# The first norm of a hybrid layer: its vector folded into the projection's weights, its row scale into the results

## The chip, the core and the metric

The kernel runs on one core of a Trainium2 chip. The time is that of the device for one execution, in microseconds (us), from the first to the last instruction and what little lies around them. The core has five engines with a queue each: TensorE (PE) for matrix products, VectorE (DVE), ScalarE (ACT), GpSimd (POOL) and SyncE (SP), which issues most of the loads.

## The reference

One layer over 1024 tokens of width 1024, all in float32. Only the first part matters here:

```
h = RMSNorm(x) * mix_norm              # per token: x * rsqrt(mean(x^2) + eps), times a vector of 1024
z = h @ W_in                           # columns: gq, gk, gv, gr, low-rank gate, sq, sk, sv
group A: gated linear attention in chunks of 64 (4 heads), per-head RMSNorm, SiLU(gr) gate
group B: sliding-window attention (window 128), per-head RMSNorm of sq and sk, ALiBi, sinks
x = x + concat([o_A, o_B]) @ W_out
x = x + W_down(SiLU(a) * b),  [a, b] = causal_conv3(RMSNorm(x) @ W_up)
```

## The kernel before

Tokens are cut into 8 tiles of 128 (index t), the width into 8 blocks of 128 (index k). Every float32 product is made of three products of rounded numbers: an operand is split into a rounded part `hi` and the difference `lo`, and TensorE adds hi\*hi, hi\*lo and lo\*hi. So a tile of a projection, `dense`, is 8 x 3 = 24 products of 128x512 into one PSUM bank. The split of a weight block is a rounding copy on ACT (`act.copy`) and a difference on POOL, or on DVE where `engs` says so; `piece` splits the two blocks of one load. The v blocks are the exception: DVE makes their rounding copy (`hi_eng`).

The opening: `load_x` brings tile t of x; `norm1_stat` squares and sums its rows on ACT (for tile 0 half of it on DVE), makes the row scale `r` (affine on DVE, power on POOL in `rms_scale`), and multiplies x by `r` and by the norm's vector in place (two DVE operations of 128x512). The vector comes as one row and is spread over the partitions by four small products into PSUM (`mix_ps`), from which ACT copies it later (`mix_copy`). `norm1_tr` transposes the normalized tile, 8 blocks by TensorE, and `norm_tr` splits the result into `big` (ACT copy, DVE difference). Then come the products of the q weights (`unit_q_part`, `unit_q`).

The stages follow each other as q, k (with the low-rank gate's columns), v, g, r, each over all 8 tiles, with the attention parts of both groups laid in between. Weight blocks live in nine slots (`w_tile`) that the stages use in turn, so that a block of the next stage can be split when the last product of an earlier stage has used its slot. Loads go through three buffers (`raw_tile`).

The order: every step is put into a list with a time by hand (`at(time, f, ...)`), and the list is run in the order of these times; the framework then places the instructions of each engine with a simulated timeline of its own, so an engine's queue can differ from the list in places. Each engine works off its queue in order.

What uses z afterwards: `q_post` and `kvl_post` (per-head norm with `head_rms`, then a multiply), a copy for the values (`kvl_post`, `unit_v`), `gla_qk` (times decays) and `gate` (SiLU).

## Time and profile before

| | us |
|---|---|
| median of 3 runs | 1093.66 (1092.42 to 1098.78) |
| the profiled execution, its own time | 1095.48 |
| its span, first to last instruction | 1093.8 |
| TensorE busy in the span | 1079.5 |
| DVE, POOL, ACT busy | 797.0, 641.5, 480.6 |

The mean granted clock of TensorE is 0.996 of full speed. All times of rows are from the profiled execution, counted from the first instruction. TensorE's busy time holds products at either clock. A line such as L89 is a line of the kernel; the lines of `split` (L86 to L89) serve all splits, so the tile's name tells which one it is (qw, kw, vw: weight blocks; big: transposed x).

### The profile page before, as it was taken

The page shows a single profiled execution, that of the slowest core. Times are in us where ns is not written, and L with a number is a line of the kernel's source. Part 1 is how long each engine was busy: PE and PEld are TensorE (multiplying, and loading weights), DVE is VectorE, ACT ScalarE, POOL GpSimd, SP SyncE. Part 2 cuts the span into 40 slices and gives each one's busy share as a digit, 9 for nine tenths or more (in the row PEclk, how much of TensorE's full clock was granted, in tenths as well). Part 3 has the DMA queues.
Part 4 walks back from the last instruction along what each step waited for, and adds up shares of the span by engine and source line. Part 5 has one row for each costly group of instructions (what it writes and reads, how often), then busy time and mean ns, then how long its engine had stood idle before and what let it go on. Part 6 is the DMA issues. An engine that isn't in the chain of part 4 may idle for free.

```text
span 1093.8 us, 14260 instructions
## 1 busy us (share of the span) xinstructions
PE 1079.5 (99%) x5156; PEld 867.3 (79%) x5156; DVE 797.0 (73%) x1323; ACT 480.6 (44%) x966; POOL 641.5 (59%) x518
## 2 busy tenths in 40 slices
PE   8999999999999999999999999999999999999998
PEld 5897778777788887878888888888888888888886
DVE  6646546767513268758898979797989798898965
ACT  6326656434332135445454444444444445454530
POOL 5356224233543237587878777786868697868530
PEclk9999999999999999999999999999999999999999
DMA  6124113000208201012211121212111111111104
GB/s 217 46 72 132 33 30 104 20 14 17 62 1 268 58 2 58 1 58 59 58 58 58 43 74 39 77 39 78 38 56 42 58 39 58 58 58 59 44 14 154
DMA packets 67344, 67.16 MB, mean 61 GB/s; under 512 B 4616, under 2 KB 51913, under 8 KB 67274
## 3 DMA queue, kind: packets, MB, share of 16 engines
q1 hardware_dynamic: 63432, 61.53, 18.1%
q10 hardware_dynamic: 3842, 4.73, 1.8%
q8 instruction: 41, 0.67, 0.3%
q14 instruction: 29, 0.24, 0.1%
HBM read 57.33 MB, written 4.19 MB: 56 GB/s over the span
## 4 chain that ended last, share of the span: by engine, by line
PE 93%; DVE 4%; DMA 1%; ACT 1%; issue 0%; POOL 0%; SPq 0%; ACTq 0%; POOLq 0%
PE fb L759 36%; PE dn_P L929 17%; PE do L288 7%; PE dg L288 4%; PE dr L288 4%; PE dv L288 4%; PE dq L288 3%; PE dk L288 2%; PE pv L449 1%; PE ppt L437 1%; PE dq L646 1%; PE X L759 1%; PE fb L960 1%; PE dl L960 1%; PE go L552 1%; PE go L548 1%
## 5 line engine op out<-in xcount | busy, mean ns | idle before, releaser
L929 PE MATMUL dn_P<-dw,dg 128*128 128x512 f32 x840 | 215.8, 392 | 0.0
L933 DVE TENSOR_TENSOR acc<-acc,dn_P 128x1024 f32<-128x1024 f32 x140 | 169.8, 1214 | 62.4 <-PE dn_P L929 62.3
L929 PEld LDWEIGHTS dn_P<-dw,dg 128*128 128x128 f32 x840 | 157.7, 188 | 37.1
L288 PE MATMUL do<-wow,big 128*128 128x512 f32 x384 | 93.2, 398 | 0.0
L89 POOL TENSOR_TENSOR dw<-dn,dw 128x512 fp32r<-128x512 f32 x50 | 69.0, 1380 | 33.0 <-PE dn_P L929 22.3
L288 PEld LDWEIGHTS do<-wow,big 128*128 128x128 f32 x384 | 71.1, 188 | 16.2
L426 POOL TENSOR_TENSOR pr<-pr,sm 128x1024 f32<-128x1024 f32 (+1 forms) x16 | 28.6, 1786 | 68.6 <-DVE sm L424 38.0
L759 PE MATMUL fb<-big,A11w 128*128 128x512 f32 x264 | 66.4, 396 | 0.0
L759 PE MATMUL fb<-big,A12w 128*128 128x512 f32 x264 | 65.6, 396 | 0.0
L767 DVE SCALAR_TENSOR_TENSOR ua<-fb,cc,ua 128x511 f32<-128x511 f32 x82 | 60.7, 741 | 4.2 <-ACT ua L772 3.7
L759 PE MATMUL fb<-big,S1w 128*128 128x512 f32 x240 | 60.0, 397 | 0.3 <-DVE ub L803 0.3
L759 PE MATMUL fb<-ex,S3w 128*128 128x512 f32 x240 | 59.7, 397 | 0.2 <-ACT ca L818 0.2
L759 PE MATMUL fb<-big,S4w 128*128 128x512 f32 x240 | 59.8, 396 | 0.0
L759 PE MATMUL fb<-ex,S2w 128*128 128x512 f32 x240 | 59.6, 396 | 0.0
L759 PE MATMUL fb<-ex,A22w 128*128 128x512 f32 x240 | 59.5, 397 | 0.0
L759 PEld LDWEIGHTS fb<-big,A11w 128*128 128x128 f32 x264 | 49.6, 188 | 12.0
L759 PEld LDWEIGHTS fb<-big,A12w 128*128 128x128 f32 x264 | 49.7, 188 | 11.7
L759 PEld LDWEIGHTS fb<-big,S1w 128*128 128x128 f32 x240 | 45.1, 188 | 11.7 <-issue 0.7
L759 PEld LDWEIGHTS fb<-ex,S3w 128*128 128x128 f32 x240 | 45.0, 188 | 11.6 <-ACT ca L818 0.9
L759 PEld LDWEIGHTS fb<-big,S4w 128*128 128x128 f32 x240 | 45.1, 188 | 11.0
L759 PEld LDWEIGHTS fb<-ex,A22w 128*128 128x128 f32 x240 | 45.1, 188 | 10.9
L759 PEld LDWEIGHTS fb<-ex,S2w 128*128 128x128 f32 x240 | 45.1, 188 | 10.9
(438 smaller groups left out, 2481.8 us busy)
## 6 DMA issues: line engine op xcount, KB each, us to landing
up<-in_w_up_dram SPq DMA_DIRECT2D x44, 512.0 KB, 3.9
dn<-in_w_down_dram SPq DMA_DIRECT2D x22, 512.0 KB, 3.5
acc<-in_x_dram SPq DMA_DIRECT2D x8, 512.0 KB, 7.5
out_dram<-acc SPq DMA_DIRECT2D x16, 256.0 KB, 2.0
xt<-in_x_dram SPq DMA_DIRECT2D x7, 512.0 KB, 4.7
qraw<-in_w_in_dram SPq DMA_DIRECT2D x4, 512.0 KB, 6.3
vraw<-in_w_in_dram SPq DMA_DIRECT2D x4, 512.0 KB, 4.2
qt<-qt ACTq DMA_DIRECT2D x16, 128.0 KB, 2.2
```

The lines of the kernel that those rows point to most:

```text
L89: (eng or pool).tensor_sub(lo, src, hi.bitcast(F32))
L288: pe.matmul(pb[:, :n], lhsT=big[:, t, k, ra, :], rhs=ws[k][:, rb, :n], start=(k == 0 and i == 0), stop=(k == KD - 1 and i == 2))
L426: pool.tensor_tensor(pr[:, :, s0:], pr[:, :, s0:], den[:, hs].rearrange("p (j o) -> p j o", o=1).broadcast_to((P, 4, n)), ALU.mult)
L437: pe.transpose(pb[:, j * P:(j + 1) * P], pr[:, j, b * P:(b + 1) * P], ident)
L449: pe.matmul(pb[g * 64:(g + 1) * 64, :], lhsT=vv[:, t - 1 + b, g * 64:(g + 1) * 64], rhs=pts[t, g][:, b, :], start=(b == b0), stop=(b == 1))
L548: pe.matmul(pb[:, h * P:(h + 1) * P], lhsT=a[:, lo, pr * P:(pr + 1) * P], rhs=v[:, h * P:(h + 1) * P], start=(h == 0), stop=False)
L552: pe.matmul(pb[c * 64:(c + 1) * 64, pr * 256:(pr + 1) * 256], lhsT=qt[:, pr, c * 64:(c + 1) * 64], rhs=s_st[(2 * t + c) % NS][:, pr, :], s ...
L759: pe.matmul(pb[:, ts.start * P:ts.stop * P], lhsT=w[:, ra, k, :], rhs=b_operand(bn, k, rb)[:, ts], start=(onto is None and i == 0), stop=( ...
L767: dve.scalar_tensor_tensor(dst, src, w, dst, op0=ALU.mult, op1=ALU.add)
L929: pe.matmul(pb[:, i], lhsT=g[:, ra, c:c + P], rhs=w[:, rb, :], start=(onto is None and n == 0), stop=(n == 2), skip_group_check=onto is no ...
L933: dve.tensor_add(acc, acc, pb)
L960: pe.matmul(pb, lhsT=g[:, ra, (t % 4) * P:(t % 4 + 1) * P], rhs=w[:, rb, :], start=(ch == NCH - 2 and i == 0), stop=(ch == NCH - 1 and i = ...
```

## The change

The rows of the weights are multiplied by the norm's vector when they are split, and the row scale of a token is multiplied into the results. x is transposed as loaded. In steps:

- the vector is loaded as `mixc`, 128 partitions x 8 numbers (number k of partition p is element 128k + p), from ACT's queue; the row, its four products and `mix_copy` go;
- `split` with `scale`: with `eng` given, ACT's rounding copy and DVE's difference both apply the scale; without, ACT first scales the loaded block in place and then splits it as before, with POOL's difference. The v blocks lose `hi_eng` and so are rounded on ACT;
- `norm1_stat` squares in place over the loaded x, after the transposes, and writes the row scale to `rn`, with `rn8` (times 1/8) and `rn2` (squared, over 64) beside it: two small DVE operations per tile. The two multiplies over the tile go;
- the results take the row scale: in `q_post`, `gla_qk`, `unit_v`, the values and the gate as a scale of an operation that was there already, in `kvl_post` for the keys by one small DVE operation more per tile. `head_rms` uses `rn2` in the affine step;
- the list's times in the opening change: transposes before statistics, the first q products in parts of two blocks.

```diff
--- before.py
+++ after.py
@@ -81,12 +81,16 @@
             return w_late["pool"].tile([P, 2, 512], F32R, tag="w9", name=name, bufs=1)
         return slot_tile(slot, name)
 
-    def split(src, hi, lo, eng=None, hi_eng=None):
-        if hi_eng is None:
+    def split(src, hi, lo, eng=None, scale=None):
+        if scale is None:
             act.copy(hi, src)
+            (eng or pool).tensor_sub(lo, src, hi.bitcast(F32))
+        elif eng is None:
+            act.activation(src, src, AF.Copy, scale=scale)
+            split(src, hi, lo)
         else:
-            hi_eng.tensor_copy(hi, src)
-        (eng or pool).tensor_sub(lo, src, hi.bitcast(F32))
+            act.activation(hi, src, AF.Copy, scale=scale)
+            eng.scalar_tensor_tensor(lo, src, scale, hi.bitcast(F32), op0=ALU.mult, op1=ALU.subtract)
 
 
     ident = idp.tile([P, P], F32, name="ident")
@@ -99,7 +103,9 @@
     sx = ExitStack()
     px = sx.enter_context(tc.tile_pool(name="px", bufs=1, side="right"))
 
-    mixn = gl.tile([P, D], F32, tag="k4", name="mixn", bufs=K4)
+
+    mixc = gl.tile([P, KD], F32, name="mixc")
+    rn, rn8, rn2 = (gl.tile([P, NT], F32, name=n) for n in ("rn", "rn8", "rn2"))
 
     dist = gl.tile([P, 256], F32, name="dist")
     slope_n = gl.tile([P, 8], F32, name="slope_n")
@@ -163,32 +169,27 @@
         for c in range(parts):
             sp.dma_start(xt[:, c * n:(c + 1) * n], x[t * P:(t + 1) * P, c * n:(c + 1) * n])
 
-    def rms_scale(ss, n, w, name, p, tag, bufs=3):
+    def rms_scale(ss, n, w, name, p, tag, bufs=3, r=None):
         v = p.tile([P, w], F32, tag=tag + "v", name=name + "v", bufs=bufs)
-        dve.tensor_scalar(v, ss, 1.0 / n, EPS, op0=ALU.mult, op1=ALU.add)
-        r = p.tile([P, w], F32, tag=tag + "r", name=name + "r", bufs=bufs)
+        dve.tensor_scalar(v, ss, n if hasattr(n, "tensor") else 1.0 / n, EPS, op0=ALU.mult, op1=ALU.add)
+        if r is None:
+            r = p.tile([P, w], F32, tag=tag + "r", name=name + "r", bufs=bufs)
         pool.tensor_tensor(r, v, mhalf[:, :w], ALU.pow)
         return r
 
     halves = (slice(0, 512), slice(512, D))
 
     def norm1_stat(t):
-        xt = xts[t]
-        junk = px.tile([P, D], F32, tag="junk", name=f"junk_{t}", bufs=1)
-        ss = px.tile([P, 2], F32, tag="n1ss", name=f"n1ss_{t}", bufs=2)
-        if t == 0:
-            act.activation(junk[:, 0:512], xt[:, 0:512], AF.Square, accum_out=ss[:, 0:1])
-            dve.tensor_tensor_reduce(junk[:, 512:], xt[:, 512:], xt[:, 512:], 1.0, ss[:, 0:1],
-                                     ALU.mult, ALU.add, ss[:, 1:2])
-        else:
-            act.activation(junk, xt, AF.Square, accum_out=ss[:, 1:2])
-        r = rms_scale(ss[:, 1:2], D, 1, f"n1{t}", px, "n1")
-        for i, c in enumerate(halves):
-            dve.scalar_tensor_tensor(xt[:, c], xt[:, c], r[:, 0:1], mixn[:, c] if t > 1 else mix_ps[i],
-                                     op0=ALU.mult, op1=ALU.mult)
+        ss = px.tile([P, 1], F32, tag="n1ss", name=f"n1ss_{t}", bufs=2)
+        xt = xts.pop(t)
+        act.activation(xt, xt, AF.Square, accum_out=ss)
+        c = slice(t, t + 1)
+        rms_scale(ss, D, 1, f"n1{t}", px, "n1", r=rn[:, c])
+        dve.tensor_scalar(rn2[:, c], rn[:, c], rn[:, c], 1.0 / HD, op0=ALU.mult, op1=ALU.mult)
+        dve.tensor_scalar(rn8[:, c], rn[:, c], 0.125, None, op0=ALU.mult)
 
     def norm1_tr(t):
-        norm_tr(t, xts.pop(t), "n1")
+        norm_tr(t, xts[t], "n1")
 
     def norm2_stat(t):
         pn, acc = fin["pn"], fin["acc"][t]
@@ -268,18 +269,18 @@
         else:
             sp.dma_start(rv, rows[:, :, c0:c0 + n])
 
-    def piece(name, n, k2, engs=(None, None), hi_eng=None):
+    def piece(name, n, k2, engs=(None, None)):
         ws = blocks.setdefault(name, [])
         rv = raws.pop((name, k2))
         for a in range(2):
             k = k2 * 2 + a
             w = w_tile(f"{name}w{k}")
-            split(rv[:, a, :], w[:, 0, :n], w[:, 1, :n], engs[a], hi_eng)
+            split(rv[:, a, :], w[:, 0, :n], w[:, 1, :n], engs[a], mixc[:, k:k + 1])
             ws.append(w)
 
-    def load_piece(name, c0, n, k2, engs=(None, None), hi_eng=None):
+    def load_piece(name, c0, n, k2, engs=(None, None)):
         raw_dma(name, c0, n, k2)
-        piece(name, n, k2, engs, hi_eng)
+        piece(name, n, k2, engs)
 
     def dense(t, ws, n, name):
         pb = bank(name)
@@ -317,18 +318,18 @@
     def k2_tile(name):
         return gl.tile([P, 512], F32, tag="k2", name=name, bufs=K2)
 
-    def head_rms(ps_ap, nh, name):
+    def head_rms(t, ps_ap, nh, name):
         sq = k2_tile(name + "sq")
         act.activation(sq[:, :nh * HD], ps_ap, AF.Square)
         ss = gl.tile([P, 8], F32, tag="hss", name=name + "ss", bufs=3)
         dve.tensor_reduce(ss[:, :nh], sq[:, :nh * HD].rearrange("p (h d) -> p h d", d=HD),
                           op=ALU.add, axis=AX.X)
-        return rms_scale(ss[:, :nh], HD, nh, name, gl, f"hr{nh}")
+        return rms_scale(ss[:, :nh], rn2[:, t:t + 1], nh, name, gl, f"hr{nh}")
 
     def q_post(t, pb):
-        r = head_rms(pb, 8, f"q{t}")
+        r = head_rms(t, pb, 8, f"q{t}")
         rs = gl.tile([P, 8], F32, tag="rs", name=f"rs{t}", bufs=2)
-        dve.tensor_mul(rs, r, qscale)
+        dve.scalar_tensor_tensor(rs, r, rn[:, t:t + 1], qscale, op0=ALU.mult, op1=ALU.mult)
         dve.tensor_tensor(
             qo[:, t, :].rearrange("p (j g d) -> p g j d", j=4, g=2),
             pb.rearrange("p (g j d) -> p g j d", g=2, j=4),
@@ -338,11 +339,13 @@
     kvl = {}
 
     def kvl_post(t, pb):
-        r = head_rms(pb[:, 0:P], 2, f"k{t}")
-        act.copy(vv[:, t, :], pb[:, P:2 * P])
+        rt = rn[:, t:t + 1]
+        r = head_rms(t, pb[:, 0:P], 2, f"k{t}")
+        dve.tensor_scalar(r, r, rt, None, op0=ALU.mult)
+        act.activation(vv[:, t, :], pb[:, P:2 * P], AF.Copy, scale=rt)
         gn = gl.tile([P, 17], F32, tag="gn", name=f"gn{t}", bufs=4)
         pool.memset(gn[:, 16:17], 1.0)
-        dve.tensor_copy(gn[:, 0:16], pb[:, 256:272])
+        dve.tensor_scalar(gn[:, 0:16], pb[:, 256:272], rt, None, op0=ALU.mult)
         kn = gl.tile([P, P], F32, tag="kn", name=f"kn{t}", bufs=4)
         dve.tensor_tensor(kn.rearrange("p (g d) -> p g d", g=2),
                           pb[:, 0:P].rearrange("p (g d) -> p g d", g=2),
@@ -490,11 +493,11 @@
         ex = gex[t]
         kz = kdz[t % 2]
         qk = k2_tile(f"qk{t}")
-        dve.scalar_tensor_tensor(qk[:, 0:256], pb[:, 0:256], 0.125, ex[:, 0], op0=ALU.mult, op1=ALU.mult)
-        dve.tensor_mul(qk[:, 256:512], pb[:, 256:512], ex[:, 1])
+        dve.scalar_tensor_tensor(qk[:, 0:256], pb[:, 0:256], rn8[:, t:t + 1], ex[:, 0], op0=ALU.mult, op1=ALU.mult)
+        dve.scalar_tensor_tensor(qk[:, 256:512], pb[:, 256:512], rn[:, t:t + 1], ex[:, 1], op0=ALU.mult, op1=ALU.mult)
         for c in range(2):
             r = slice(c * 64, (c + 1) * 64)
-            dve.tensor_mul(kz[r, c, :], pb[r, 256:512], ex[r, 2])
+            dve.scalar_tensor_tensor(kz[r, c, :], pb[r, 256:512], rn[r, t:t + 1], ex[r, 2], op0=ALU.mult, op1=ALU.mult)
         gqk[t] = qk
 
     def gla_tr(t):
@@ -561,7 +564,7 @@
 
     def gate(t, pb):
         gs = k2_tile(f"gs{t}")
-        act.activation(gs, pb, AF.Silu)
+        act.activation(gs, pb, AF.Silu, scale=rn[:, t:t + 1])
         pool.tensor_mul(vg[0][:, t, :].rearrange("p (h d) -> p h d", h=4), vg[0][:, t, :].rearrange("p (h d) -> p h d", h=4),
                         grs[t].rearrange("p (h o) -> p h o", o=1).broadcast_to((P, 4, P)))
         pool.tensor_mul(gs, gs, vg[0][:, t, :])
@@ -655,7 +658,7 @@
         kvl_post(t, dense(t, blocks["k"], 272, f"dk{t}"))
 
     def unit_v(t):
-        act.copy(vg[0][:, t, :], dense(t, blocks["v"], 512, f"dv{t}"))
+        act.activation(vg[0][:, t, :], dense(t, blocks["v"], 512, f"dv{t}"), AF.Copy, scale=rn[:, t:t + 1])
 
     def unit_g(t):
         gla_qk(t, dense(t, blocks["g"], 512, f"dg{t}"))
@@ -969,20 +972,8 @@
     def at(time, f, *a):
         ev.append((time, len(ev), f, a))
 
-    mix_row = k4_tile("mix_row")[0:1, :]
-    ones = k2_tile("ones")[0:1, 0:P]
-    dve.memset(ones, 1.0)
-    act.dma_start(mix_row, mix_norm)
+    act.dma_start(mixc, mix_norm.rearrange("o (k p) -> p (o k)", p=P))
     load_x(0, 2)
-    mix_ps = []
-    for c in halves:
-        pb = bank(f"mix{len(mix_ps)}")
-        pe.matmul(pb, lhsT=ones, rhs=mix_row[:, c], start=True, stop=True)
-        mix_ps.append(pb)
-
-    def mix_copy():
-        for c, pb in zip(halves, mix_ps):
-            act.copy(mixn[:, c], pb)
 
     TQ, TK, TV, TG, TR, TO = 0.0, 8.0, 12.8, 20.8, 28.8, 36.8
     TU = TO + 16.0
@@ -992,27 +983,27 @@
     raw_dma("q", CSQ, 512, 2)
     raw_dma("q", CSQ, 512, 3)
     load_x(2)
-    at(-9.0, norm1_stat, 0)
+    at(-9.0, norm1_tr, 0)
     at(-8.9, piece, "q", 512, 0, (None, dve))
-    at(-8.8, norm1_tr, 0)
-    at(-8.7, piece, "q", 512, 1, (None, dve))
-    at(-8.6, unit_q_part, 0, 0, 4)
-    at(-8.22, mix_copy)
-    at(-8.5, norm1_stat, 1)
-    at(-8.4, norm1_tr, 1)
+    at(-8.8, unit_q_part, 0, 0, 2)
+    at(-8.7, norm1_tr, 1)
+    at(-8.65, piece, "q", 512, 1, (None, dve))
+    at(-8.6, unit_q_part, 0, 2, 4)
     at(-8.3, piece, "q", 512, 2, (None, dve))
+    at(-8.27, norm1_stat, 0)
     at(-8.25, unit_q_part, 0, 4, 6)
     at(-8.2, unit_q_part, 1, 0, 6)
     at(-8.15, piece, "q", 512, 3, (None, dve))
-    at(-8.1, norm1_stat, 2)
+    at(-8.12, norm1_tr, 2)
+    at(-8.1, norm1_stat, 1)
     at(-8.0, unit_q_part, 0, 6, 8)
-    at(-7.95, norm1_tr, 2)
+    at(-7.95, norm1_stat, 2)
     at(-7.9, unit_q_part, 1, 6, 8)
     for t in range(NT):
         if t > 1:
             if t > 2:
                 at(t - 2.7, load_x, t)
-                at(t - 2.5, norm1_stat, t)
+                at(t - 1.5, norm1_stat, t)
             if t > 2:
                 at(t - 1.6, norm1_tr, t)
             at(TQ + t, unit_q, t)
@@ -1034,7 +1025,7 @@
     for i in range(4):
         d = 0.2 * i
         at(TK - 0.9 + d, load_piece, "k", 0, 272, i)
-        at(TV - 0.9 + d, load_piece, "v", CV, 512, i, (None, None), dve)
+        at(TV - 0.9 + d, load_piece, "v", CV, 512, i, (None, None))
         at(TG - 0.9 + d, load_piece, "g", CQ, 512, i, (None, dve))
         at(TR - 0.9 + d, load_piece, "r", CR, 512, i, (None, dve))
         at(TO - 0.9 + d, load_wo, "o0", 0, i)
```

## Rows read from the trace of the kernel before

**Rows 1.** The page's first part: busy time, share, instructions of each engine

```profile
PE 1079.5 (99%) x5156; PEld 867.3 (79%) x5156; DVE 797.0 (73%) x1323; ACT 480.6 (44%) x966; POOL 641.5 (59%) x518
```

**Rows 2.** TensorE's waits over the span: total us, times, longest us

```profile
PE mix L980 <- DMA mix_row<-in_mix_norm_dram: 3.0, 1, 3.0
...
PE n1pt L246 <- DVE n11v L168: 1.9, 1, 1.9
PE kpt L356 <- DVE kn L347: 1.3, 1, 1.3
```

**Rows 3.** The chain of waits, 0 to 30 us: start, us, what

```profile
1.71 5.12 DMA qraw<-in_w_in_dram
...
6.85 1.15 ACT qw L86 x2
...
10.10 1.09 PE n1pt L246 x4
11.19 2.99 PE dq L646 x7
...
15.88 7.69 PE dq L646 x33
23.57 0.87 PE n1pt L246 x8
```

**Rows 4.** The timeline, 0 to 22: start, us, engine, line [idle before <-releaser]

```profile
2.96 3.75 PE L980 MATMUL mix<-mix_row,ones 1*128 1x512 f32 x4 [2.96 <-DMA mix_row<-in_mix_norm_dram]
...
3.56 0.63 ACT L180 ACTIVATE junk<-xt 128x512 f32<-128x512 f32 x1 [1.48 <-DMA xt<-in_x_dram]
...
4.57 0.75 DVE L181 CUSTOM_DVE_ANT_0 junk<-xt,n1ss 128x512 f32<-128x512 f32 x1 [2.84 <-DMA xt<-in_x_dram]
...
8.23 1.06 ACT L184 ACTIVATE junk<-xt 128x1024 f32<-128x1024 f32 x1 [0.24 <-DMA xt<-in_x_dram]
```

**Rows 5.** The q weights' tile: issues (ns, then first and last us), landing

```profile
L269 SPq DMA_DIRECT2D qraw<-in_w_in_dram x4: 433/698/928, 1.7 to 4.2; - x4
...
DMA to landing us min/median/max: 5.1/6.3/8.1
```

**Rows 6.** Groups on ACT and DVE, 0 to 345: busy us, mean ns

```profile
L249 ACT CAST big<-n1pt 128x512 fp32r<-128x512 f32 x16 | 8.7, 587 | 0.9 <-PE n1pt L246 0.9
...
L576 ACT ACTIVATE big<-ogt,glan 128x512 fp32r<-128x512 f32 x8 | 5.5, 686 | 6.3 <-PE ogt L573 6.3
...
L86 ACT CAST qw<-qraw 128x512 fp32r<-128x512 f32 x8 | 4.6, 623 | 2.6 <-DMA qraw<-in_w_in_dram 2.6
...
L250 DVE TENSOR_TENSOR big<-n1pt,big 128x512 fp32r<-128x512 f32 x16 | 10.6, 683 | 0.4 <-ACT big L249 0.4
...
L577 DVE SCALAR_TENSOR_TENSOR big<-ogt,glan,big 128x512 fp32r<-128x512 f32 x8 | 6.0, 750 | 30.2 <-ACT big L576 30.2
...
L88 DVE CAST vw<-vraw 128x512 fp32r<-128x512 f32 x8 | 3.0, 410 | 1.5 <-DMA vraw<-in_w_in_dram 1.5
...
L168 DVE TENSOR_SCALAR g4v<-gss 128x4 f32<-128x4 f32 x1 | 0.2, 171 | 0.0
```

**Rows 7.** Stretches: us, busy PE, PEld, DVE, ACT, POOL; clock; DMA

```profile
64.00:88.00 24.00, 24.00 (x186) 22.94 (x185) 11.75 (x38) 8.47 (x29) 9.65 (x16) 1.00 0.34 95
88.00:104.00 16.00, 14.68 (x81) 11.33 (x80) 14.19 (x50) 11.64 (x42) 13.61 (x12) 0.97 0.48 134
```

**Rows 8.** The timeline around the seam, POOL, then DVE, then PE

```profile
61.83 4.42 POOL L89 TENSOR_TENSOR kw<-kraw,kw 128x272 fp32r<-128x272 f32 x6
...
92.01 6.27 POOL L89 TENSOR_TENSOR vw<-vraw,vw 128x512 fp32r<-128x512 f32 x5
...
100.30 2.50 POOL L89 TENSOR_TENSOR vw<-vraw,vw 128x512 fp32r<-128x512 f32 x2
...
96.98 1.33 DVE L168 TENSOR_SCALAR k7v<-k7ss 128x2 f32<-128x2 f32 x1
...
101.94 4.58 PE L288 MATMUL dv<-vw,big 128*128 128x512 f32 x12
```

## The prediction

> **What bounds the kernel now.** The first thing to read is the page's table of engines: TensorE is busy for 1079.5 of 1093.8 us [rows 1]. No change that leaves the products alone can give back more than the remaining 14.3 us, and one per cent of the kernel is 10.9 us. I count one per cent as about what a measurement of this kernel can tell from no change. So the question is which part of those 14.3 us the edit can reach.
>
> TensorE's list of waits answers it. The long ones that this edit touches are 3.0 us at the very start, 1.9 us before four transposes of x, and 1.3 us at the end of the k stage [rows 2]. The first two lie in the opening, and the chain of waits shows what the opening consists of [rows 3]: the first weights land at 6.83 (5.12 us after 1.71), ACT splits them, and the first product starts only at 11.19, because four transposes wait behind a normalization until 10.10. Seven products then take 2.99 us, 427 ns each, which is 512 columns at 1.2 GHz, the lower of the two clock levels. From 15.88 on 33 products take 7.69 us, 233 ns each, and the q stage has no idle TensorE time afterwards. **So the opening decides, and its measure is how much full-speed work is done when the steady stream begins.** By 15.88 TensorE has done 10 products and 16 transposes. At full speed that is 10 x 0.233 plus 16 x 0.109 (eight transposes in 0.87 [rows 3]), 4.1 us. The opening thus costs 15.88 - 4.1 = 11.8 us.
>
> **The change, part by part.**
>
> *Transposes without the norm.* Removed from the path are the row sum of squares, the power on POOL and the two DVE multiplies per tile. The halves of x are there when ACT and DVE take them up, at 3.56 and 4.57 [rows 4]. Eight transposes at the low clock take 2.2 us (four in 1.09 [rows 3]), so they end about 5.8. The ACT copy of the last half (0.59) and the DVE difference (0.68 [rows 6]) make the first tile ready at 7.1, before any weight can be. All of this lies in TensorE's present idle time. The four small products that spread the vector, 2.96 to 6.71 [rows 4], also go, but nothing waits for TensorE there.
>
> *Weights with the scale.* Each pair of q blocks now costs ACT an in-place scaling, a rounding copy, and a rounding copy with scale. A scale held per partition makes a 128x512 activation 0.69 instead of 0.59, 0.10 more [rows 6]. Added to the 0.62 of the rounding copy from SBUF this is 0.72, 0.62, 0.72, or 2.06. Starts follow closer than durations (two copies take 1.15, not 1.24 [rows 3]), so I take 1.9 a pair against 1.15 now. Block 0: scaling and copy end at 8.1, POOL's difference (1.25 each: five in 6.27 [rows 8]) ends at 9.4. Block 1: its copy ends at 8.7 and the DVE difference, now with scale (0.75 [rows 6]), at 9.5. The first product can start at 8.1 instead of 11.19.
>
> *The next late thing is ACT.* Three pairs are 5.7 us, the copies of the second x tile (there at 8.23 [rows 4]) 1.2. From 6.85 that makes 13.7 for block 5, and with the last difference 14.5. The weights themselves are on time: the last of the four loads is issued at 4.2 and lands at most 8.1 later, at 12.3 [rows 5]. TensorE by then can do 12 products and 16 transposes. At full speed these are 12 x 0.233 + 16 x 0.109 = 4.5 us, and the opening costs 14.5 - 4.5 = 10.0 us. The gain is 11.8 - 10.0 = 1.8 us. If the clock rises no sooner than now, three of the 12 products end at 14.9 and the gain is 1.4. If ACT is no hindrance, the whole 11.19 - 8.1 = 3.1 is gained. Blocks 6 and 7 wait on ACT for the square of tile 0 (1.06 [rows 4]) and come at 13.7 + 1.1 + 1.9 + 0.75, about 17.5. They are covered by 24 products of other blocks, 5.6 us from 14.5. I take 1.8, with 0 and 3.1 as ends.
>
> *The vector's load.* It was one row of 4 KB, there by 2.96 [rows 4]. Now it is 128 partitions of eight numbers, each from its own address, on ACT's queue. The trace has no such load. Everything that scales a weight waits for it, behind it on ACT the whole split of q, and behind that TensorE. It has until 6.83. Taken: on time, 0. Upper end: it lands as long after its issue at 0.83 as the slowest weight load, 8.1 [rows 5], at 8.9, which is 2.1 late and eats the gain. It can't gain, as the split could not start before the weights land.
> Here a rule speaks against the change. The Trainium skill ("DMA: Bandwidth & Descriptors", Rules for kernel authors) says that a last dimension that is not contiguous becomes one descriptor per element, and asks for another arrangement. By that rule this load is 1,024 pieces of 4 bytes, in turn with x and the weights. The trace can't settle it, as it holds no load of so many pieces. By the rule, taken at that end, the forecast would be 1093.7 and not 1091.9.
>
> *Statistics, moved.* Square, DVE affine and POOL power per tile now come behind the transposes; two DVE operations per tile are added, two 0.75 multiplies go. Who needs the scale first is the q result of tile 0, after its 24 products; that is later than the square by several us, so no wait. A buffer of x is now freed by the square and not by the transposes, and the SP queue holds the next x load until then, with the k weights queued behind it. The next x is needed two units later (48 products, 11.2 us), a load lands within 8.1 us [rows 5], and the k weights' differences run only at 61.83 [rows 8]: taken at 0. Each us by which the square ends more than 3.1 later than the transposes do now would be a us of waiting.
>
> *Blocks k, v, g, r.* k gains eight in-place scalings. POOL, with six differences in a row from 61.83 to 66.25 [rows 8], is later than ACT there, which is nearly free: 0, at most 1 if the last pair lands late. v's rounding moves from DVE (eight of 0.41) to ACT and gets a scaling in front, 8 x (0.72 + 0.62) = 10.7 us more on ACT. g and r have four more scalings each; the list of waits names none at their starts, so 0, and at most 1.4 each, two scalings uncovered.
>
> *The seam from k to v.* In the stages that the edit touches this is the longest later wait of TensorE. The transpose of the last k tile waited 1.3 us [rows 2], and the twelve v products behind it took 4.58 instead of 2.80 [rows 8], with a granted clock of 0.97 in the mean over 88 to 104 [rows 7]: 1.8 us lost to the lower level. For v products the last two differences of POOL, 100.30 to 102.80, are as late as the k tile [rows 8]. The edit takes DVE casts off that chain and adds a small multiply to it. The small DVE operation at 96.98 took 1.33 [rows 8] where its like elsewhere takes 0.17 [rows 6], while POOL was at its run of differences. So the added multiply costs 0.17 to 1.3 and the casts give back 0 to 2.9 (seven of 0.41 [rows 6]). With POOL's differences as the next late thing I take the seam at 0, with ends of -3.1 (wait and low clock both gone) and +6.8 (below).
> The Trainium skill ("SBUF — State Buffer", Who interferes with whom) has a rule for this: DVE instructions in the two-port mode or with two SBUF inputs share a port pair with POOL, and the one that starts second waits for all of the other, while ACT never waits. The 1.33 us agree. By the rule alone the move to ACT would help the seam, and the forecast would go towards 1088.8.
>
> All other edits (scale operands in the results' epilogues, an activation in place of a copy) change one operation into another of the same shape, at most 0.10 each on ACT, while TensorE works on the next tile.
>
> **Sum.** The profiled execution took 1095.48 us, of which the span is 1093.8; it lies 1.8 above the median of the three runs, 1093.66. The gain of 1.8 in the opening (by chance the same figure) makes 1095.5 - 1.8 = 1093.7 of the profiled execution, and **1091.9 us** of the median, which I predict.
>
> **The rivals.**
> *The seam heals.* With the casts gone from DVE, the last k tile is early, TensorE's pause shrinks and the clock stays up. Against it: POOL's differences end at 102.8 whatever DVE does, unless ACT delivers sooner. Result 1091.9 - 1.3 - 1.8 = 1088.8.
> *No gain in the opening.* The vector lands at 8.9, or the issue order puts the copies of x behind the weights, so that the edit doesn't do what it says. For it: the scattered load. Against it: four us of slack. Result 1093.7.
> *ACT becomes late at the seam: slower.* Seven of v's blocks are split between 88 and 104, as their slots come free from q and k. ACT then has 9.4 us more (7 x 1.34) and only 16 - 11.64 = 4.4 us free [rows 7], a lack of 5.0 us for which the v products wait, and a low clock of 1.8 that lasts longer by as much again. 1091.9 + 5.0 + 1.8 = 1098.7. It decides from the point at which fewer than seven in-place scalings (7 x 0.72 = 5.0) run before 88. They need no slot, only the loaded weights, and ACT is free for 24 - 8.47 = 15.5 us in 64 to 88 [rows 7], which speaks against; at least the two blocks of the last load can't come early, which speaks for.
>
> **How the numbers follow.** The forecast case, opening gain with nothing else moved: 0.50, with its own range 1090 to 1093.5. Seam heals: 0.17. No gain: 0.13. ACT late: 0.13. Something else, above all another issue order between 60 and 340 where all engines feed each other, 0.07, more of it slower than faster. From 1087.5 to 1098 the first three cases lie inside, and half of the ACT case. Over one per cent faster (below 1082.7) would need nearly all of TensorE's idle time: 0.02. Over one per cent slower (above 1104.6): a seam twice as bad as worked out, 0.04. Within: 0.94.
>
> **What would show it.** Right: transposes of x from about 3.6, a first q product near 8, steady 233 ns from 14 to 15, no mix products, ACT nearly full from 7 to 17. If the first scaling on ACT starts well after 6.85, the vector was late. At the seam: whether in-place scalings of v stand before 88, when the last v difference ends (now 102.8), and the granted clock in 88 to 108. The forecast is wrong if TensorE's idle time outside the first 15 us changes by more than 2 us.

## The result and the profile after

The median is 1099.3 us after the change (1096.7 to 1106.0, 22 runs) against 1096.3 before (1092.4 to 1101.8, 22 runs); the ratio is 1.0038, interval 1.0022 to 1.0053. The change makes the kernel slower by 0.4 per cent: little, but beyond the uncertainty, on the other side of the forecast and above its range (1087.5 to 1098).

The profiled execution took 1099.55 us with a span of 1097.8, 4.0 more than before. The first place to look is where TensorE's stages begin, which the timeline shows as the first product of each. The first k product comes at 62.3 (63.5 before), the first g product at 171.5 (170.8), the first r product at 279.6 (276.1), the end of the last product at 1093.9 (1089.9). So the opening gains 1.2, the stretch from k to g loses 1.9 (109.2 against 107.3), the one from g to r 2.7 (108.1 against 105.4), and the rest 0.5.

The page's first part and TensorE's waits of the changed kernel answer to [rows 1, 2]:

```profile
PE 1079.1 (98%) x5152; PEld 867.6 (79%) x5152; DVE 786.8 (72%) x1320; ACT 501.7 (46%) x1000; POOL 639.9 (58%) x518
```

```profile
PE n1pt L247 <- DMA xt<-in_x_dram: 6.0, 2, 4.3
...
PE dv L289 <- ACT vw L86: 2.0, 1, 2.0
PE kpt L359 <- DVE kn L350: 1.1, 1, 1.1
PE fb L762 <- DVE ub L806: 1.1, 1, 1.1
```

The waits for the normalized tile of x are gone. New is one of 2.0 us for a block of v that ACT rounds; that for DVE's last k tile (`kn`) has shrunk only from 1.3 to 1.1. The first wait of the FFN for its operand was 0.3 before; that covers the 0.5 at the end.

The opening on TensorE and ACT (timeline, 4 to 16) answers to [rows 3, 4]:

```profile
4.31 2.14 PE L247 MATMUL n1pt<-ident,xt 128*128 128x128 f32 x8 [4.31 <-DMA xt<-in_x_dram]
...
6.97 1.06 ACT L185 ACTIVATE xt<-xt 128x1024 f32<-128x1024 f32 x1
...
8.02 0.71 ACT L89 ACTIVATE qraw<-qraw,mixc 128x512 f32<-128x512 f32 x1
...
8.16 1.11 PE L247 MATMUL n1pt<-ident,xt 128*128 128x128 f32 x4 [1.71 <-DMA xt<-in_x_dram]
...
9.90 0.79 PE L649 MATMUL dq<-qw,big 128*128 128x512 f32 x1 [0.63 <-ACT qw L86]
```

The first scaling starts at 8.02 and not at 6.85, since tile 0's square stands ahead of it in ACT's queue; the first product starts at 9.90 and not at 8.1, after a wait for ACT's first rounded block. (The timeline of before has its first product at 10.84; the 11.19 of [rows 3] is where the step of the chain begins.)

The seam from k to v, all engines in order of time, answers to [rows 8]:

```profile
96.82 0.71 ACT L89 ACTIVATE vraw<-vraw,mixc 128x512 f32<-128x512 f32 x1
...
97.18 1.22 DVE L344 TENSOR_SCALAR k7r<-k7r,rn 128x2 f32<-128x2 f32 x1 [0.77 <-POOL k7r L177]
...
97.94 0.72 ACT L89 ACTIVATE vraw<-vraw,mixc 128x512 f32<-128x512 f32 x1
...
98.78 0.33 PE L359 MATMUL kpt<-ident,kn 128*128 128x128 f32 x1 [1.14 <-DVE kn L350]
...
98.97 0.71 PE L289 MATMUL dv<-vw,big 128*128 128x512 f32 x2
...
100.13 0.71 ACT L89 ACTIVATE graw<-graw,mixc 128x512 f32<-128x512 f32 x1
...
100.99 0.61 ACT L86 CAST vw<-vraw 128x512 fp32r<-128x512 f32 x1
...
101.66 0.61 ACT L86 CAST vw<-vraw 128x512 fp32r<-128x512 f32 x1
101.66 0.50 PE L289 MATMUL dv<-vw,big 128*128 128x512 f32 x1 [1.97 <-ACT vw L86]
101.73 2.51 POOL L87 TENSOR_TENSOR vw<-vraw,vw 128x512 fp32r<-128x512 f32 x2 [1.74 <-ACT vw L86]
```

Six of v's eight in-place scalings had run before 88. The last two run at 96.82 and 97.94, but their roundings come only at 100.99 and 101.66: between them ACT's queue holds results of the k and q tiles and even a scaling of g's first weights. TensorE stands still until 101.66, and POOL's last differences end at 104.24 (102.80 before).

The same in stretches of 4 us (PE, PEld, DVE, ACT, POOL busy; clock; DMA), answering to the second of [rows 7]:

```profile
96.00:100.00 4.00, 2.55 (x11) 1.24 (x9) 3.09 (x7) 3.90 (x13) 3.42 (x4) 1.00 0.64 155
100.00:104.00 4.00, 2.34 (x6) 1.58 (x7) 0.68 (x2) 2.95 (x8) 2.27 (x2) 0.83 0.83 220
104.00:108.00 4.00, 4.00 (x14) 3.19 (x14) 1.48 (x4) 3.02 (x8) 2.19 (x6) 0.74 0.57 155
```

and before:

```profile
96.00:100.00 4.00, 3.62 (x16) 2.16 (x14) 3.94 (x9) 2.89 (x12) 3.83 (x4) 1.00 0.69 180
100.00:104.00 4.00, 3.05 (x11) 2.13 (x12) 2.94 (x8) 3.39 (x9) 4.00 (x5) 0.88 0.74 218
```

From 96 to 104 TensorE is busy for 4.89 us of 8; before it was 6.67. ACT is nearly full until 100 and then has gaps, so it is the order of its queue more than its load that makes it late. After the pause the clock falls: the trace's clock record has 3.4 us at the lower level (1.2 GHz) from 102.65, which costs 1.7 us. The profile of before has as much from 103.05.

That record matters for all that follows. Between opening and end, a stretch at the lower level lasted 3.4 or 6.8 us wherever a profile of this case shows one (those of e1 and e12 show none), and costs half of that. The changed kernel's second one, from 194.8, is 1.7 of the 2.7 us lost between g and r. I therefore compare stages with these halves taken off. Of the 35 runs of the kernel before in the second set of experiments 11 show a mean clock of 1.00; of the changed kernel's 34 runs none is above 0.997.

### The profile page after: what moved, and what is told of

It reads as the page before. It is cut to its first block, busy times and chain, and to the rows that moved or that the text cites. A ratio compares the mean times of both kernels' runs of the same rounds, so it can differ in the third digit from the quotient of the medians.

```text
span 1097.8 us, 14249 instructions
## 1 busy us (share of the span) xinstructions
PE 1079.1 (98%) x5152; PEld 867.6 (79%) x5152; DVE 786.8 (72%) x1320; ACT 501.7 (46%) x1000; POOL 639.9 (58%) x518
## 2 busy tenths in 40 slices
DMA packets 68382, 67.16 MB, mean 61 GB/s; under 512 B 5655, under 2 KB 52952, under 8 KB 68312
## 4 chain that ended last, share of the span: by engine, by line
PE 85%; DVE 3%; ACT 1%; DMA 1%; issue 0%; POOL 0%; ACTq 0%; DVEq 0%; POOLq 0%
PE fb L762 36%; PE dn_P L932 17%; PE do L289 7%; PE dg L289 4%; PE dr L289 4%; PE dv L289 4%; PE pv L452 1%; PE ppt L440 1%; PE X L762 1%; PE fb L963 1%; PE dl L963 1%; PE go L555 1%; PE go L551 1%; DVE n2h L204 1%; DMA dn<-in_w_down_dram 1%; PE ga L540 1%
## 5 line engine op out<-in xcount | busy, mean ns | idle before, releaser
L936 DVE TENSOR_TENSOR acc<-acc,dn_P 128x1024 f32<-128x1024 f32 x140 | 169.8, 1214 | 62.4 <-PE dn_P L932 62.3
```

The source lines that it names most:

```text
L936: dve.tensor_add(acc, acc, pb)
```

## The experiments

All in one table. First products are read from each profile; "low" is the time at the lower clock between the first k and the first g product, and between g and r; the last two columns are these stretches less half of it. The first k product also depends on the low clock of the opening, which lasts until 12.0 us in e13 and until 15.9 in e12; its start moves by half of such a difference. The kernel before had medians of 1095.8, 1095.6, 1095.7 and 1095.4 us beside the four sets (e0 to e3, e4 to e7, e8 to e11, e12 to e14). In the expectations S is the theory of v's roundings in ACT's queue; O is a loss elsewhere in e0 to e3 and, from e11 on, the order of TensorE's queue.

| kernel | median (lowest) | ratio, interval | first k, g, r | low | k to g | g to r |
|---|---|---|---|---|---|---|
| before | 1096.3 (1092.4) | | 63.5, 170.8, 276.1 | 3.4, 0 | 105.6 | 105.4 |
| after | 1099.3 (1096.7) | 1.0038, 1.0022-1.0053 | 62.3, 171.5, 279.6 | 3.4, 3.4 | 107.5 | 106.4 |
| e0 | 1098.6 (1096.6) | 1.0040, 1.0020-1.0059 | 62.0, 172.8, 279.4 | 6.8, 0 | 107.4 | 106.6 |
| e1 | 1092.9 (1091.9) | 0.9994, 0.9972-1.0017 | 62.9, 168.4, 274.9 | 0, 0 | 105.5 | 106.6 |
| e2 | 1094.5 (1092.0) | 0.9989, 0.9969-1.0009 | 61.5, 167.1, 275.1 | 0, 3.4 | 105.6 | 106.4 |
| e3 | 1103.3 (1097.3) | 1.0058, 1.0037-1.0079 | 64.0, 174.5, 279.8 | 6.8, 0 | 107.1 | 105.4 |
| e4 | 1096.3 (1093.8) | 1.0007, 0.9989-1.0025 | 62.5, 171.4, 277.9 | 3.4, 0 | 107.1 | 106.6 |
| e5 | 1094.0 (1091.4) | 0.9982, 0.9967-0.9997 | 62.3, 167.7, 274.7 | 0, 3.4 | 105.4 | 105.2 |
| e6 | 1097.8 (1093.3) | 1.0008, 0.9989-1.0026 | 62.1, 167.1, 275.1 | 0, 3.4 | 105.0 | 106.4 |
| e7 | 1092.9 (1091.5) | 0.9977, 0.9961-0.9993 | 62.3, 167.7, 274.6 | 0, 3.4 | 105.4 | 105.2 |
| e8 | 1095.1 (1091.7) | 0.9993, 0.9969-1.0017 | 62.9, 168.0, 275.0 | 0, 3.4 | 105.1 | 105.3 |
| e9 | 1098.3 (1097.1) | 1.0013, 0.9997-1.0029 | 62.4, 172.5, 277.9 | 6.8, 0 | 106.7 | 105.4 |
| e10 | 1097.4 (1094.2) | 1.0006, 0.9985-1.0027 | 61.4, 168.6, 274.0 | 0, 0 | 107.2 | 105.4 |
| e11 | 1096.5 (1095.0) | 1.0003, 0.9986-1.0019 | 62.3, 169.0, 275.5 | 0, 0 | 106.6 | 106.5 |
| e12 | 1095.1 (1093.6) | 0.9990, 0.9971-1.0009 | 63.3, 169.3, 275.8 | 0, 0 | 105.9 | 106.5 |
| e13 | 1094.9 (1090.9) | 0.9985, 0.9963-1.0007 | 61.6, 167.5, 272.9 | 0, 0 | 105.9 | 105.4 |
| e14 | 1097.3 (1093.2) | 1.0008, 0.9985-1.0030 | 62.7, 170.4, 276.1 | 3.4, 0 | 106.0 | 105.7 |

**e0, the change again.**

> The changed kernel a second time, to see how far its stages move between executions. Both theories: first k product near 62.3 us, first g product near 171.5, first product of r near 279.6, ratio to before about 1.004. If the low-clock stretch near 195 us of the first profile is missing here, the r products start about 1.7 earlier, and that part of the loss is a matter of the single execution.

It came out as in the first comparison, and both of its stretches agree with it once the low clock is taken off.

**e1, v rounded by DVE again**, still scaled in place by ACT:

```diff
-            split(rv[:, a, :], w[:, 0, :n], w[:, 1, :n], engs[a], mixc[:, k:k + 1])
+            if name == "v":
+                src = rv[:, a, :]
+                act.activation(src, src, AF.Copy, scale=mixc[:, k:k + 1])
+                dve.tensor_copy(w[:, 0, :n], src)
+                pool.tensor_sub(w[:, 1, :n], src, w[:, 0, :n].bitcast(F32))
+            else:
+                split(rv[:, a, :], w[:, 0, :n], w[:, 1, :n], engs[a], mixc[:, k:k + 1])
```

> The changed kernel with the rounding of the v blocks back on DVE; their in-place scaling stays on ACT. Theory S (the seam: v's last roundings stand in ACT's queue behind attention work, so the last v weights are late): from the first k product to the first g product 107 us again instead of 109.2, the last v difference on POOL ends before 102.8, ratio to before 0.999 to 1.002. Theory O (the loss is elsewhere: row scales in the results, or the order in the g stage): k to g stays at 109.2, ratio 1.004.

The loss from k to g is gone, against the theory that puts it elsewhere. TensorE's waits at the seam are 0.3 us for v and 0.5 us for the low-rank gate (`gt` of `kvl_tr`), which ACT copies.

**e2, no vector in the weights** (plain splits, v rounded by DVE; the norm's vector is left out):

> The changed kernel with no scaling of the weights at all: the norm's vector is left out of the computation (its load stays), v's rounding is on DVE as before. What is left is the move of the statistics and the row scales in the results. Theory S: the full gain of the opening and no loss after: first k product at 61 to 62.3 (before: 63.5), k to g 107.3, ratio 0.996 to 0.999. Theory O: the loss stays without any weight scaling, ratio at least 1.003.

From k to g it takes 105.6 against e1's 105.5, and the intervals of the two ratios overlap almost wholly. The scalings themselves cost nothing that shows.

**e3, the kernel before with ACT's scaling and rounding of v alone:**

```diff
+            if name == "v":
+                act.activation(rv[:, a, :], rv[:, a, :], AF.Copy, scale=one)
+                split(rv[:, a, :], w[:, 0, :n], w[:, 1, :n])
...
```

> The kernel before with only the v blocks handled as in the change: scaled in place on ACT (by a column of ones) and rounded on ACT instead of DVE. Theory S: k to g goes from 107.3 to about 109, the last v difference ends after 103.5, ratio 1.001 to 1.003, with the opening as before (first k product 63.5). Theory O: no change, ratio 1.000.

This edit by itself makes the loss: k to g takes 107.1 at full clock, TensorE waits 1.9 us for ACT's rounding, and the clock is low for 6.8 us behind it. The ratio, 1.0058, is above what the theory allowed; the profile also has a later first k product (64.0) and a wait of 3.9 us in the FFN with a low clock behind it. From g to r it takes 105.4 as before, so the 1.0 to 1.2 us lost there are another matter.

**e4 and e11, which of v's roundings.** In e4 DVE rounds only the last two blocks, in e11 only the first six.

```diff
-            if name == "v":
+            if name == "v" and k >= 6:     (e4; in e11: k < 6)
```

> The changed kernel with only the last two of v's eight blocks (k = 6, 7) rounded by DVE; the first six are rounded by ACT as in the change, all eight are scaled in place by ACT. Theory S (the loss is the place of the last two roundings in ACT's queue, 100.99 and 101.66 in the profile of the changed kernel, with POOL's last two differences behind them): TensorE's wait of 2.0 us for v's blocks falls below 0.7 us, from the first k product to the first g product it takes 105.5 to 107 us instead of 109.2, and the median comes to that of the kernel in which DVE rounds all eight, 1092 to 1095. Rival A (the amount of ACT's work in the stage is the cause, wherever it stands in the queue): six of the eight roundings are still ACT's, three quarters of the loss stays, the wait is 1.5 us or more and the median 1096 to 1098.

> The complement of the variant with the last two blocks on DVE: the changed kernel with v's first six blocks rounded by DVE and the last two (k = 6, 7) by ACT, all eight scaled in place by ACT; the pv products as in the change. That variant took 1.3 us less than the change where no other low clock fell into it, and 1.3 more than with all eight on DVE; TensorE waited 1.55 us for POOL's difference of the last pair and 1.14 for the last k tile. Theory S: the last two roundings come at 100 to 102 again, TensorE waits 1.5 to 2.5 us for v, the median is 1096 to 1099. Theory O (the order of the other six roundings decides, through the order of TensorE's queue, in which the last k tile's transposes and the products of the last pair come sooner than with all eight on DVE): the wait is under 1 us and the median 1092.5 to 1095.5.

Their waits on TensorE, first e4:

```profile
PE dv L295 <- POOL vw L282: 1.6, 1, 1.6
PE kpt L365 <- DVE kn L356: 1.1, 1, 1.1
```

and e11:

```profile
PE sc L414 <- ACT vg L667: 1.2, 1, 1.2
...
PE dv L295 <- ACT vw L86: 0.7, 1, 0.7
```

My theory of the last two roundings fell in its narrow form. With them on DVE, TensorE waits for POOL's difference of one of these blocks instead, 107.1 in all; with the other six on DVE it waits only 0.7 us for ACT, in spite of the last two blocks being ACT's. So it doesn't matter by itself which engine rounds the last two. The order of TensorE's instructions in the changed kernel, as built, shows what is left (vw_1196 is v's sixth block, vw_1202 the seventh; dv_1250 and dv_1314 are the first two tiles of v):

```
207 L289 MATMUL dv_1250<-vw_1196,big 128x512 x2
208 L289 MATMUL dv_1250<-vw_1202,big 128x512
209 L376 MATMUL za_1295<-wa,gt_1188 128x256
210 L289 MATMUL dv_1314<-vw_1084,big 128x512 x3
...
215 L289 MATMUL dv_1314<-vw_1196,big 128x512 x3
```

One product on the seventh block, the one that waits 1.97 us above, stands ahead of 18 of the next tile (4.2 us at 233 ns) that need only blocks long since ready.

This order is not new, however. As built, the kernel before, e1, e3 and e11 have one such product in the same place, ahead of the same 18. What differs is when ACT or DVE rounds the seventh block. Counted from the first k product to the start of that rounding, with TensorE's wait for it:

| kernel | rounding starts after | wait |
|---|---|---|
| before (DVE) | 34.9 | none |
| e1 (DVE) | 35.8 | 0.3 |
| e11 (ACT) | 36.0 | 0.7 |
| e3 (ACT) | 37.8 | 1.9 |
| changed (ACT) | 38.7 | 2.0 |

So the lateness of the rounding in its engine's queue is one half of the wait. e4 shows the other half, the order of the products: its rounding is hardly later than e1's (36.4), but four products on the last two blocks stand ahead of ready ones there, and it waits 1.6 us for POOL.

**e12, another order of these products.** ACT rounds v as in the change; the first two v tiles are given out in two parts, by a step `v_part` that is to `unit_v` what `unit_q_part` is to `unit_q`:

```diff
-        at(TV + t, unit_v, t)
+        if t < 2:
+            at(TV - 0.28 + 0.05 * t, v_part, t, 0, 6)
+            at(TV + 0.05 * t, v_part, t, 6, 8)
+        else:
+            at(TV + t, unit_v, t)
```

> The changed kernel with ACT's roundings as the change has them; only the products of the first two v tiles are given out in two parts, all 36 on the first six blocks ahead of the 12 on the last two. Theory O (the loss at the seam is that a product on block 6 stands in TensorE's queue ahead of 18 that are ready, so that ACT's late rounding stops them all): from 99 to 104 TensorE has work while ACT rounds the last blocks, its waits for v's blocks and the last k tile come to under 1.0 us (3.1 in the change), and from the first k product to the first g product it takes 105.5 to 106.3 us without a low clock (107.4 in the change, 105.6 before, 105.4 with v rounded by DVE); the median is 1094 to 1097. Theory A (ACT has too much work there, whatever the order): the waits only move, to the results of v and the scores that wait for ACT, and the stretch stays at 107 or more.

Its stretches at the seam:

```profile
96.00:100.00 4.00, 4.00 (x20) 3.23 (x20) 3.90 (x13) 3.95 (x13) 3.85 (x4) 1.00 0.53 145
100.00:104.00 4.00, 4.00 (x20) 2.90 (x19) 3.33 (x7) 3.98 (x13) 2.69 (x3) 1.00 0.53 162
104.00:108.00 4.00, 4.00 (x20) 2.89 (x20) 1.48 (x3) 2.42 (x6) 3.00 (x10) 1.00 0.61 182
```

TensorE has no pause there though ACT is no less busy, the clock stays up, k to g takes 105.9 instead of 107.5, and the median falls by some 3.5 us against e0. So the loss is one of order and not of ACT's amount of work. But the edit changed more than TensorE's order: the framework, which places all engines, also gave out ACT's last two roundings sooner (timeline):

```profile
97.92 0.62 ACT L86 CAST vw<-vraw 128x512 fp32r<-128x512 f32 x1
...
100.00 0.60 ACT L86 CAST vw<-vraw 128x512 fp32r<-128x512 f32 x1
```

These are 34.6 and 36.7 us after the first k product, where the changed kernel has 38.7 and 39.3. e12 alone therefore doesn't tell the two queues apart. By an estimate from these rows TensorE's new order would have been enough: at the old distances the two roundings would end at 102.6 and 103.3, and e12's first products on these blocks start at 103.6 and 105.0; POOL's differences would end at 104.0 and 105.3 and are first used at 104.1 and 105.5. No run has this new order with ACT's old one. Under 0.4 us are left against the kernel before; they may lie in two later waits, 0.6 and 0.4 us, for the low-rank gate that ACT copies.

**e5, e13, e14: the g stage.** In all kernels so far with the row scale in the results (e2 has it, e3 has not), g to r takes 106.4 to 106.6. TensorE there (timeline), in the changed kernel:

```profile
261.18 1.07 PE L452 MATMUL pv<-pt,vv 128*64 128x512 f32 x2
262.18 0.66 PE L507 MATMUL gt<-ident,qk 128*128 128x128 f32 x4
262.77 1.93 PE L452 MATMUL pv<-pt,vv 128*64 128x512 f32 x6
264.63 1.09 PE L440 MATMUL ppt<-ident,pr 128*128 128x128 f32 x8
```

and before:

```profile
258.83 1.94 PE L449 MATMUL pv<-pt,vv 128*64 128x512 f32 x8
260.70 0.44 PE L437 MATMUL ppt<-ident,pr 128*128 128x128 f32 x2
```

The eight pv instructions of a tile took 1.87 us in one piece, start to start, and 1.00 + 1.86 in two, with the transposes of gt between them. No list of waits shows this. In e5 (on top of e1) and e13 (on top of e12) these transposes are given out later; e14 is e5 with the order of e12.

```diff
-        at(s + 1.0, gla_tr, t)
+        at(s + (1.5 if t == 5 else 1.0), gla_tr, t)
```

> The changed kernel with v rounded by DVE, and in addition the transposes of one tile's gated q and k (tile 5) given out half a unit later, so that in TensorE's queue they no longer stand between the products of one tile's attention output (pv), which run in pairs on two halves of the columns. Theory G: in the changed kernel and in all its variants the stretch from the first g product to the first r product is 1.2 to 1.3 us longer than in the kernel before (106.6 against 105.3 where no low clock falls into it), and about 1.0 of this is the split pair: the eight pv instructions of that tile take 2.87 us in two pieces and 1.87 in one. It then falls to 105.4 to 105.8, and the median lies 0.5 to 1.5 below that of the kernel with v rounded by DVE alone. Rival: the longer operations with a scale on DVE (0.48 instead of 0.42 us, 0.97 instead of 0.85) are the cause; the stretch stays at 106.4 to 106.7.

> As the last one, with the pv products of one tile also left whole. Theory O with G: the change itself, with two orders mended, has from k to g 105.5 to 106.3 and from g to r 105.3 us, and with the opening's gain the time of a run without a low clock is 1091 to 1092.3, the median 1092 to 1096. Theory A: the median stays at 1096 to 1098.

> The same two orders mended, with v rounded by DVE. If ACT's roundings cost something of their own beside the order, this is 0.5 us or more faster than the last one from k to g; by theory O alone the two agree within 0.3 us there. Against the variant with v on DVE and the pv products whole (105.4 from k to g, median 1094.0) it should gain at most 0.4 us, since that one waits 0.8 us at the seam.

In e5:

```profile
257.51 1.94 PE L458 MATMUL pv<-pt,vv 128*64 128x512 f32 x8
259.38 0.55 PE L513 MATMUL gt<-ident,qk 128*128 128x128 f32 x3
```

The stretch falls to 105.2 in e5 and 105.4 in e13, as before the change, and to 105.7 in e14; the longer operations with a scale on DVE cost nothing there that shows. e13 and e14 agree from k to g within 0.1, but e14 holds a wait of 1.7 us for the low-rank gate that e13 has not, and e5, DVE's rounding in the old order, takes 105.4 against e13's 105.9. That ACT's rounding costs nothing of its own is therefore not shown; by these stretches it is some 0.5 us at most. e14's median is the worse one, and its clock fell once more, from 110.4, behind that wait.

**e9 and e10, other engines for v** (on top of e5):

```diff
-        at(TV - 0.9 + d, load_piece, "v", CV, 512, i, (None, None))
+        at(TV - 0.9 + d, load_piece, "v", CV, 512, i, (dve, dve))     (e9; in e10: (None, dve))
```

> The variant with the pv products left whole, but v's eight blocks each made by two instructions: a rounding copy with scale on ACT and a scaled difference on DVE; no in-place scaling, nothing on POOL. ACT then has 8 x 0.72 = 5.8 us for v where the change gave it 10.7, DVE 8 x 0.75 = 6.0 us. Theory P (beside ACT's queue it is POOL, with differences of 1.25 us that end at 102.7 to 104.2, that keeps v's blocks from TensorE): TensorE's waits for v's blocks and the last k tile come to under 0.6 us together, from the first k product to the first g product 105.0 to 105.6, and the time of a run without a low clock is 1090.5 to 1091.5. Rival D (DVE becomes the late one: 6 us more between 88 and 104, with the k tile's chain on the same engine): the wait of the last k tile grows to 1.5 us or more and the time is 1092.5 or more.

> As the last one, but v's blocks made as g's and r's are: of each pair one block by in-place scaling, rounding on ACT and a difference on POOL, the other by a rounding with scale on ACT and a scaled difference on DVE. ACT has 4 x (0.72 + 0.62) + 4 x 0.72 = 8.2 us, POOL four differences (5.0), DVE 3.0. Theory S in its wider form (ACT's queue at the seam holds the rounding of the last block with an in-place scaling, k = 6, behind other work): TensorE still waits 1 to 2 us for v, less than in the change, and the time of a run without a low clock after the opening lies at 1091.5 to 1093.5, between the variants. Rival P: with POOL's work halved nothing is late, waits under 0.6 us, 1090.5 to 1091.5.

Both miss. With POOL out of it (e9) the wait moves on, to the scores behind ACT's copy of a result of v:

```profile
PE sc L408 <- ACT vg L661: 2.2, 1, 2.2
```

The waits for v's blocks are gone without POOL, but the stage is no shorter, and neither theory had named this wait. Scores read nothing of v: as built, they go into the PSUM bank that the first v tile holds until ACT has copied it. In e10 TensorE waits 1.2 us for v's blocks (0.9 of it for POOL), as theory S said, and 0.5 for the low-rank gate, but k to g is 107.2, and its fastest run, 1094.2, lies above that theory's times.

**e6, e7, e8: the opening** (on top of e1). e6 loads the vector as eight rows and transposes it; e7 adds e5's order and takes tile 0's square on DVE; e8 also gives the second tile of x out behind the third weight load.

```diff
-    act.dma_start(mixc, mix_norm.rearrange("o (k p) -> p (o k)", p=P))
+    act.dma_start(mix8, mix_norm.rearrange("o (k p) -> (o k) p", p=P))
+    pe.transpose(mpt[:, 0:KD], mix8, ident[:KD, :KD])
+    dve.tensor_copy(mixc, mpt[:, 0:KD])
...
+        if t == 0:
+            dve.tensor_tensor_reduce(xt, xt, xt, 1.0, zero, ALU.mult, ALU.add, ss)
...
-    load_x(1)
     raw_dma("q", CSQ, 512, 1)
     raw_dma("q", CSQ, 512, 2)
+    load_x(1)
```

> The changed kernel with v rounded by DVE, and the norm's vector loaded as eight rows of 512 bytes and turned into columns by one TensorE transpose and one DVE copy, in place of the load of 1,024 single numbers. Theory V (the scattered load holds up the transfers of x beside it): the second half of x's first tile, for which its transposes start at 5.24 to 5.48 in the four profiles with the scattered load, is there at 4.6 to 4.9, ACT's square and first scaling move up by as much, and the first q product starts 0.3 to 0.6 earlier than 9.9 to 10.0, at 9.4 to 9.7. Rival Q (what holds up the first product is ACT alone, with the square of tile 0 ahead of the first scaling, and the weights' landing): the first q product stays at 9.8 or later. The median falls by 0.5 at most by either.

> All in one: v rounded by DVE, the pv products of a tile left whole, the vector loaded as eight rows, and the sum of squares of tile 0 taken by DVE, so that ACT's first scaling stands right behind the copies of the first x tile. Theory (each loss is separate and they add up): the first scaling starts at 6.8 to 7.2 instead of 8.0 to 8.2, the first q product at 8.7 to 9.2 instead of 9.9 to 10.0, the k stage's first product at 61.5 to 62.2, the g stage 105.4 to 105.8, and in a run without a low clock after the opening the time is 1090 to 1091 against 1092.5 of both the kernel before and the variant with v on DVE; median 1090 to 1093, ratio 0.996 to 0.999. Rival: the time given back in one place is waited for in the next, or the low clock falls more often, and the median stays at 1093 to 1096.

> The variant with all four repairs, and the load of x's second tile given out behind the third weight load of q and no longer between the first and the second; its eight transposes then stand behind the first seven products in TensorE's queue and not ahead of the first. Theory X (TensorE's first product waits, in its queue, behind the transposes of x's second tile, and these for its landing: 2.26 us, until 8.72, in the variant with all repairs, where ACT's first rounded block would allow it at 8.8): the first product starts at 8.3 to 8.9 instead of 9.49, and the stretch until the k stage shrinks by 0.3 to 0.6 (k start less half of the moment at which the clock rises: 55.5 in that variant, 56.3 before, 55.1 to 55.4 in the others). Rival: the steady stream then waits for the second tile or for ACT's later blocks instead, and the k stage starts no sooner; the first product may still be earlier.

e6 did not bring the first product forward (9.97). In e7 ACT's first scaling starts at 6.97, near the 6.85 of the forecast, and TensorE now waits for the second tile of x, whose transposes stand ahead of the first product:

```profile
8.72 1.12 PE L252 MATMUL n1pt<-ident,xt 128*128 128x128 f32 x4 [2.26 <-DMA xt<-in_x_dram]
9.49 0.78 PE L660 MATMUL dq<-qw,big 128*128 128x512 f32 x1
```

In e8 the first product starts at 8.40, and the next block is late:

```profile
8.40 0.79 PE L660 MATMUL dq<-qw,big 128*128 128x512 f32 x1 [2.41 <-ACT qw L86]
10.18 2.93 PE L660 MATMUL dq<-qw,big 128*128 128x512 f32 x6 [0.98 <-POOL qw L87]
```

The k stage starts at 62.3 and 62.9, no sooner than in e1 to e5. The first product can move by 1.5 us without moving the end of the opening. e5 and e7 are the only versions whose interval lies below the kernel before, by 0.2 per cent; that e7 adds something to e5 is not shown.

## Why the prediction was wrong

**The step that failed is "the seam from k to v", taken at 0.** It measured +1.9 us at full clock (107.5 against 105.6), a wait of 2.0 us for v's seventh block behind ACT's queue, where the prediction had POOL's differences as the next late thing. The rival "ACT becomes late at the seam", given 0.13 and 1098.7, names the mechanism that occurred: v products waiting for ACT's rounding, a pause, a low clock. I had set it aside because in-place scalings would run early, and six of them did. But the products need the rounding behind the scaling, and two things that I had not worked out decided: the roundings' place in ACT's queue, and the place of one product in TensorE's. The first was new, the second was there before. The rival's price was wrong too: not 5.0 us of missing ACT time, but a wait of 2.0 us, and then the clock. That its 1098.7 lies so near 1099.3 is luck. That figure and the forecast both start from the median of three runs, 1093.66, and over 22 runs the kernel before has 1096.3: of the 7.4 us between 1091.9 and 1099.3, 2.6 are that.

**The low clock** I had taken as 1.8 us, present before and possibly healed. The kernel before escapes it in some of its runs, the changed kernel in none of 34; e12, without the pause, escapes it in its profile. Part comes back later: in e2 and e5 to e8 the clock holds at the seam and falls between 190 and 192 instead, behind a wait of 0.7 us that every profile has there.

**That other edits cost at most 0.10 each** held for the operations and missed the order. The row-scale edits (e2 has them, e3 not) led to another order of TensorE's instructions, 1.0 to 1.2 us dearer between g and r. I had this only as "something else", at 0.07.

**The opening** was sized 1.8 and gave 1.2, of which some 0.2 is an earlier rise of the clock (at 13.9 us against 14.3, half speed until then). The vector was on time as taken: by the list of DMA issues it landed 3.8 us after its issue at 0.8, well before ACT's first scaling at 8.02.

```profile
mixc<-in_mix_norm_dram ACTq DMA_DIRECT2D x1, 4.0 KB, 3.8
```

The term that was mis-sized is the chain to the first product (8.1 forecast, 9.90; ACT's square of tile 0 came ahead of the first scaling and not behind the third pair), but e7 and e8 show that this isn't what sets the end. In e8 the last pair of q blocks is scaled from 12.01, right after its weights have landed; that the fourth load sets the end is likely and was not tried.

**DVE relieved** came true: the last k tile was made at 98.43 instead of 100.60, and the added multiply took 1.22 us beside POOL's differences, within the bounds of 0.17 to 1.3. It brought nothing, because TensorE's queue then held the late v product next. The wait beside it (1.3 us before, 1.1 after), which the prediction gives to the transpose of the last k tile, belongs to another: one more k tile is transposed after it, at 111.30 in the kernel before and at 112.75 in the changed one.

```profile
111.30 0.27 PE L356 MATMUL kpt<-ident,kn 128*128 128x128 f32 x1
```

```profile
112.75 0.33 PE L359 MATMUL kpt<-ident,kn 128*128 128x128 f32 x1
```

As built, what waits is the transpose of the seventh tile, because it goes into the PSUM bank that holds the eighth tile's result until DVE has made `kn` from it. In e11 these two have different banks, and the wait is not in its list.

The Trainium skill ("SBUF — State Buffer", Who interferes with whom) would have had the move to ACT help here; the port rule agrees with the 1.22 us (the multiply ended at 98.40, POOL's difference beside it at 98.38), but a rule on one engine's delays says nothing on what stands in the queues. By the Trainium skill's rule ("DMA: Bandwidth & Descriptors", Rules for kernel authors) the vector is 1,024 pieces, and the profile agrees: its page counts 5655 transfers under 512 bytes and 4616 before. Yet no run shows a time that it cost: with eight rows in its place (e6) the first product came no sooner.

**Statistics, k, g and r blocks, q blocks 6 and 7**, all taken at 0: no wait of theirs is in the list.

## What to carry to other kernels

A piece of work that is moved to an engine with free time is late or not by its place in that engine's queue, and what it costs is decided by what stands behind the instruction that waits for it. Before moving work, write down for the consumer which of its next instructions don't need the moved result: here 18 products were ready behind one that wasn't, and giving them out first gave back most of what the move had cost, without moving anything back (the framework shifted ACT's queue along with them). When a wait names a tile that the waiting instruction doesn't read, look for the PSUM bank they share. Compare variants by stage with the low-clock time taken off, since one pause more or less moves the whole run by 1.7 us or 3.4.
